# Recurrence steps on a common table of times, two clamps on GpSimd, and other first PSUM banks, in a one-core decoder layer

## The chip, the cores and the metric

The kernel runs on one core of a Trainium2 chip. A core has TensorE (PE, matmuls), VectorE (DVE), ScalarE (ACT), GpSimd (POOL) and SyncE (SP, which here starts transfers), each with its own queue of instructions that it works off in order; an instruction whose semaphore is not yet set holds up everything behind it in that queue. Matmul results land in PSUM banks of 128 x 512 float32, everything else lives in SBUF. The metric is the device time of one execution in microseconds (us). The kernel before takes 1142.49 us (median of 3 runs, 1142.37 to 1142.78).

## The reference

One layer of a hybrid decoder on a sequence of 1024 positions with 1024 channels, in float32: norm, one combined input projection, eight heads of dilated attention beside four heads of a gated linear recurrence (HGRN2), an output projection with a residual, and a gated MLP with a short convolution. The change is in the recurrence and in the projections that feed it:

```python
def hgrn2_mixer(q, f, i, lb):              # 4 heads, 128 wide, chunks of 64
    qf = silu(q)
    forget = lb + (1 - lb) * sigmoid(f)
    key, log_f = 1 - forget, log(forget)
    b = cumsum(log_f)                      # within a chunk
    q_dec, k_inv = qf * exp(b), key * exp(-b)
    A = tril(einsum(q_dec, k_inv))         # scores within a chunk
    o_intra = einsum(A, iv)
    k_end = key * exp(b_end - b)
    U = einsum(k_end, iv)                  # what a chunk adds to the state
    state = decay * state + U              # from chunk to chunk
    o_inter = einsum(q_dec, state)
    return o_intra + o_inter
```

The result is normalised per head, multiplied by a gate `silu(g)`, and goes with the attention's result into the output projection.

## The kernel before

**Products.** Each wide matrix product is made of three matmuls on a high and a low part of both operands (lines L514, L515, L516: high x high, low x high, high x low), with a 128 x 512 result. A pair of output tiles is made of seven such products (`pair_block`), by a scheme in the manner of Strassen's with sums of operands (names T1 to T4, B11, B21, B22). `product` yields a credit of 0.65 us for each three matmuls, and a filler (`fill.run(us)`) issues three at a time until the credit is used up. PE's program order is thus written by hand: what a step issues on PE stands where the filler had come to when the step was called. The order of the other engines' instructions is chosen by the framework's scheduler.

**First attention blocks.** The products for queries and keys (`qk_block`, evacuated by the copy L542 and the sums L544 to L556, then multiplied by a norm's row at L718 into `kp` and `qp`) are followed by scores `S` (L788), in groups of small matmuls between the wide ones; L797 applies the mask and takes the maximum of a score tile. `block_banks` names the PSUM bank that each product takes: `mm` in turn for the blocks from the second on. The banks have names by use (`mm`, `s`, `o`, `t`), each with its buffers.

**Recurrences.** Eight of them run: head h and half hf of the sequence, in the order (0,0), (0,1), (1,0), (1,1), (2,0), (3,0), (2,1), (3,1). While they run, the filler issues the wide products of the remaining projections and of the output projection. Each has five steps with wishes for time in a list `steps`, in units of 5.2 us of filler's credit:

1. start: `B`, the logarithm `A`, the running sum `C` (L1027), exponentials; `E` becomes q_dec and `B` k_inv. No matmul.
2. `psK` (L1044, four transposes of B into bank `t`, copied by ACT at L1052 into `kT`) and `psA` (L1049, L1050, eight narrow matmuls into bank `s`), masked by DVE at L1054 into `AT`.
3. `psU` (L1060, bank `s`), then the states: L1062, L1067, L1071 on DVE and L1068, L1072 on ACT; for hf 0 the last state is copied by POOL (`carry`, L1075).
4. `psO` (L1083, L1085, bank `o`), sums of squares (L1089, ACT), a reciprocal root (`rstd_part`: L369, L370, L371 on ACT, L372, L373 on DVE) and `on` (L1092, DVE).
5. `psT` (L1098, four transposes of `on` into bank `t`), then the gate's multiplication G (L1100, DVE).

I call what stands on PE between two wide matmuls a visit. Beside the recurrences a step `attn_stat` runs once for each half: four loads with squares (L968) and sums (L970), then, 4.0 units later, the sum `ass` over the partitions (L973, into a bank `t`) with `rstd_part` on it (so L369 and L372 there work on 128 x 512).

**Gates.** `q_out` and `g_last` evacuate q and the gate: a clamp at -40 into the tile `F` (L921, L928 on DVE), three ACT rows of a sigmoid on `F` (L859, L860, L861), and a multiplication on DVE (L923, L930). `F` has one buffer, so these chains follow each other one at a time.

Of the kernel before, what the change touches and what calls it, by code (L numbers as in the profile page):

```python
# [3 lines left out]

# [25 lines left out]
SHARED = 4  # L30
BIG = 1e30
PARTS = (13.2, 15.8)
STARTS = (1.7, 4.6, 7.6, 10.8, 14, 17, 19.4, 22.0)
SPLIT = 24.5
END = 27.8
STAT = (3.5, 6.8)
STAGES_AT = (1.8, 2.9, 4.1, 5.5)
PARKED = (5,)
PARK_I = (3, 4, 5, 5, 5, 6, 6, 6)

# [224 lines left out]
def hybrid_kernel(ctx: ExitStack, tc: tile.TileContext, xT, w_qk, w_tok, w_hg, w_out, w_up,  # L265
                  w_down, vecs, amask, hmask, out):
    nc = tc.nc
    PE, DVE, ACT, POOL = nc.tensor, nc.vector, nc.scalar, nc.gpsimd
# [132 lines left out]
    def bank(tag, name):  # L401
        return ps1.tile([P, H2], F32, tag=tag, name=name, bufs=2)
# [4 lines left out]
    at = at_cm.__enter__()  # L407
# [14 lines left out]
    def vtile(name):  # L422
        return at.tile([P, H2], F32, tag="vi", name=name, bufs=4)
# [135 lines left out]
    blocks, block_banks = [], [cycle(("mm",))]  # L559
# [136 lines left out]
    for t in TURN:  # L696
        x = vtile(f"it{t}")
        tok_out(ivd, t, x, V[t])

    def run(g):  # L700
        for _ in g:
            pass
# [18 lines left out]
    def qk_block(p):  # L721
        return pair_block(("qk", p), lambda m, hf: mtile(f"u{p}_{m}{hf}"), qk_evac(p))
# [7 lines left out]
    for hf in range(2):  # L730
        rms1_row(hf)
    run(first)
    block_banks[0] = cycle(("mm",))
    fill.add(*[qk_block(p) for p in range(1, 4)])
    fill.run(3.9)
    xp_cm.__exit__(None, None, None)
# [5 lines left out]
    if True:  # L742
# [29 lines left out]
        def scores(p, b):  # L772

            qp, kp = qk[p]
            far = 32 * max(b - 1, 0)
            near = P if b == 0 else 2 * P
            k0 = (b + 1) * P - near
            n = far + near
            S = [bank(("so" if b % 2 else "ss")[e], f"S{p}_{b}_{e}") for e in range(2)]
            rows = [slice(64 * e, 64 * e + 64) for e in range(2)]  # L780
            k4 = kp.rearrange("p (b r l) -> p r b l", r=4, l=32)
            for part in range(2 if far else 1):
                for r in range(4):
                    o = slice(32 * r, 32 * r + 32)
                    for e in range(2):
                        q = qp[rows[e], b * P + 32 * r : b * P + 32 * r + 32]
                        if part == 0:
                            PE.matmul(S[e][o, far:n], q, kp[rows[e], k0 : k0 + near], start=True, stop=True)  # L788
                        else:
                            PE.matmul(S[e][o, 0:far].rearrange("p (b l) -> p b l", l=32), q,  # L790
                                      k4[rows[e], r, 0 : b - 1], start=True, stop=True)
            m = mask[:, FAR - far :] if b else mask[:, FAR + P :]
            Ps = probs[p, b] = []
            for e in range(2):
                Pt = ab.tile([P, FAR + NEAR], F32, tag=f"P{e}", name=f"P{p}_{b}_{e}", bufs=3)
                st = at.tile([P, 16], F32, tag="st", name=f"st{p}_{b}_{e}", bufs=8)
                DVE.tensor_tensor_reduce(Pt[:, :n], S[e][:, :n], m, -(DH ** -0.5), BIG * 3,  # L797
                                         op0=ALU.add, op1=ALU.min, accum_out=st[:, 0:1])
                ACT.activation(Pt[:, :n], Pt[:, :n], AF.Exp, bias=st[:, 0:1], scale=-1.0, accum_out=st[:, 2:3])  # L799
                DVE.reciprocal(st[:, 3:4], st[:, 2:3])  # L800
                POOL.tensor_scalar(Pt[:, :n], Pt[:, :n], st[:, 3:4], 1.0, op0=ALU.mult, op1=ALU.mult)  # L801
                Ps.append(Pt)
# [55 lines left out]
        def sigmoid(dst, src):  # L858
            ACT.activation(dst, src, AF.Exp, scale=-1.0)  # L859
            ACT.activation(dst, dst, AF.Ln, bias=1.0)  # L860
            ACT.activation(dst, dst, AF.Exp, scale=-1.0)  # L861
# [17 lines left out]
        for x in slots[:LAG]:  # L879
            scores(*x)  # L880
            fill.run(1.5)
# [19 lines left out]
    with pool("hg", "right") as hg:  # L901
# [3 lines left out]
        def ht(tag, nm, bufs=1):  # L905
            return hg.tile([P, H2], F32, tag=tag, name=nm, bufs=bufs)
# [3 lines left out]
        def tile_of(kind, h, hf):  # L910
            tag, bufs = {"hf": ("A", 4), "hq": ("E", 5), "hg": ("GH"[h // 2], 4)}[kind]
            return ht(tag, f"{tag}{h}_{hf}", bufs)
# [5 lines left out]

        def q_out(h, hf, E):
            F = ht("F", f"F{h}_{hf}")  # L920
            DVE.tensor_scalar_max(F, E, -40.0)  # L921
            sigmoid(F, F)
            DVE.tensor_mul(E, E, F)  # L923
            gate.setdefault((h, hf), {}).update(E=E)

        def g_last(h, hf, g_):
            F = ht("F", f"Fg{h}_{hf}")
            DVE.tensor_scalar_max(F, g_, -40.0)  # L928
            sigmoid(F, F)
            DVE.tensor_mul(g_, g_, F)  # L930
            G[h, hf] = g_
# [31 lines left out]
        def attn_stat(hf):  # L963
            acc = ht("H", f"asq{hf}", 4)
            for c in range(4):
                x = ar[c % 2]
                nc.sync.dma_start(x, rawd[c, hf])
                ACT.activation(x if c else acc, x, AF.Square)  # L968
                if c:
                    DVE.tensor_add(acc, acc, x)  # L970
            yield
            ss = bank("t", f"ass{hf}")
            PE.matmul(ss, ones, acc, start=True, stop=True)  # L973
            R2.append(rstd_part(ht("R", f"R2_{hf}", 2), acc, ss, 1.0 / 512))
            yield

        def attn_parts(hf):
            hi, lo = spare(f"attn{hf}")
            for c in range(4):
                a = ring.raw(rawd[c, hf])  # L980
                DVE.scalar_tensor_tensor(a, a, col(V_AG + c), R2[hf], op0=ALU.mult, op1=ALU.mult)
                ACT.copy(hi[:, c], a)
                DVE.tensor_sub(lo[:, c], a, f32(hi[:, c]))
            return hi, lo
# [16 lines left out]
        for hf in range(2):  # L1001
            for kind, h in HG[0]:
                x = tile_of(kind, h, hf)
# [12 lines left out]
        def recur(h, hf):  # L1016
            A, E = (gate[h, hf].pop(x) for x in "AE")
            nm = f"{h}_{hf}"
# [18 lines left out]
            DVE.tensor_mul(E, E, C)  # L1037
            DVE.tensor_mul(B, B, A)
            yield
            psA = bank("s", f"psA{nm}")  # L1040
            psK = bank("t", f"psK{nm}")
            for c in range(4):
                s = slice(c * P, (c + 1) * P)
                PE.transpose(psK[:, s], B[:, s], ident)  # L1044


            for c in range(4):
                s, s1, s2 = slice(c * P, (c + 1) * P), slice(c * P, c * P + 64), slice(c * P + 64, (c + 1) * P)
                PE.matmul(psA[0:64, s], B[:, s1], E[:, s], start=True, stop=True)  # L1049
                PE.matmul(psA[64:128, s], B[:, s2], E[:, s2].unsqueeze(1).to_broadcast([P, 2, 64]), start=True, stop=True)  # L1050
            kT = ht("kT", f"kT{nm}")
            ACT.copy(kT, psK)  # L1052
            pA3 = psA.rearrange("p (c t) -> p c t", c=4)
            DVE.copy_predicated(AT, hm.unsqueeze(1).to_broadcast([P, 4, P]), pA3)  # L1054
            yield
# [2 lines left out]
            for c in range(n):  # L1058
                s = slice(c * P, (c + 1) * P)
# [4 lines left out]
            st = ht("rs_y", f"st{nm}").rearrange("p (c t) -> p c t", c=4)  # L1064
# [15 lines left out]
            for c in range(4):  # L1080
                s = slice(c * P, (c + 1) * P)
# [4 lines left out]
            sq, ss = ht("rs_m", f"hsq{nm}"), hg.tile([P, 12], F32, tag="sm", name=f"hss{nm}", bufs=2)  # L1086
            for c in range(4):
                s = slice(c * P, (c + 1) * P)
# [7 lines left out]
            for c in range(4):  # L1096
                s = slice(c * P, (c + 1) * P)
                PE.transpose(psT[:, s], on[:, s], ident)  # L1098
            g_ = G[h, hf]
# [6 lines left out]
        def split_rec(hf):  # L1106
            hi, lo = rec_parts[hf] = spare(f"rec{hf}")
            for h in range(NG):
                g_ = G.pop((h, hf))
                ACT.copy(hi[:, h], g_)  # L1110
                DVE.tensor_sub(lo[:, h], g_, f32(hi[:, h]))
# [13 lines left out]
        steps = []  # L1125
        attn_ops = {}

        def rec_steps(h, hf):
            chain = iter(())

            def first():
                nonlocal chain
                chain = recur(h, hf)
                next(chain)

            yield first
            while True:
                yield lambda: next(chain, None)

        for (h, hf), start in zip(((0, 0), (0, 1), (1, 0), (1, 1), (2, 0), (3, 0), (2, 1), (3, 1)),  # L1140
                                STARTS):
            steps += zip((start, *(start + x for x in STAGES_AT)), rec_steps(h, hf))
        for hf in range(2):
            stat = attn_stat(hf)
            steps += [(STAT[hf] + x, lambda stat=stat: next(stat, None)) for x in (0, 4.0)]
            steps.append((PARTS[hf], lambda hf=hf: attn_ops.update({hf: attn_parts(hf)})))
# [4 lines left out]
        def play(end):  # L1151

            nonlocal done
            while steps and steps[0][0] < end:
                at, f = steps.pop(0)
                fill.run(5.2 * (at - done))
                done = at
                f()
            fill.run(5.2 * (end - done))
            done = end  # L1160
# [55 lines left out]
        fill.add(*[out_block(*x) for x in OUT_BLOCKS[0]])  # L1216
        play(SPLIT)
        split_rec(0)
# [196 lines left out]
    with pool("ps2", "left", space=PSUM) as ps2:  # L1415
# [162 lines left out]
        for x, y in STAGES:  # L1578
# [11 lines left out]
            for k in range(NPAIR):  # L1590
                hi, lo = ring.get((("dn", x), k))
                ahi, alo = feed.get((y, k))
                for d in range(KS):
                    s = slice(d * P, (d + 1) * P)
# [102 lines left out]
```

## Time and profile before

| | |
|---|---|
| median of 3 runs | 1142.49 us |
| the profiled execution's own time | 1142.57 us |
| its span in the trace | 1140.6 us |
| PE, busy | 1127.5 us, 6404 matmuls |
| DVE, busy | 970.2 us |
| ACT, busy | 580.6 us |
| POOL, busy | 89.9 us |
| mean granted TensorE clock | 0.998 |

The span runs from the first to the last instruction that the profiler recorded; 1.97 us of the execution's own time lie around it. Busy time is the sum over an engine's instructions. Idle time of an engine that nothing waits for costs nothing. A line of a timeline gives start and length in us, the engine, the line of the kernel, the operation, out<-in, the tile's partitions x elements, how often, and in brackets how long the engine had been idle before it and what ended that.

### The profile page before, as it was taken

Reading aid. Unit: us, or ns where it says so; the run is one execution under the profiler, and the core shown is the slowest. Engines: PE = TensorE matmul, PEld = TensorE weight load, DVE = VectorE, ACT = ScalarE, POOL = GpSimd, SP = SyncE. Lnnn points to the kernel's source line nnn. Section 1 sums busy time; section 2 is a strip of 40 time slices with the busy share of each in tenths; the row PEclk is TensorE's granted clock in tenths of the full one; section 3 lists DMA queues with packets and bytes.
Section 4 is the critical chain, followed back from the end, with each engine's and each line's share of the span. In section 5 each row is a group of like instructions: output and inputs, shape, how many; then the busy total and the mean of one; then the engine's idle time right before and its main releaser. Section 6 shows DMA issues by size and latency. Waiting matters only on the chain.

```text
span 1140.6 us, 17940 instructions
## 1 busy us (share of the span) xinstructions
PE 1127.5 (99%) x6404; PEld 927.4 (81%) x6404; DVE 970.2 (85%) x1768; ACT 580.6 (51%) x1151; POOL 89.9 (8%) x107
## 2 busy tenths in 40 slices
PE   9999999999999999999999999999999999999996
PEld 8888677778878888888788888888888888888885
DVE  7687977778999985989999999888988789857987
ACT  7545545465788665564433434343434444444553
POOL 5200333330000002000000000000000000000000
PEclk9999999999999999999999999999999999999999
DMA  7147322224315542311233223322332376435532
GB/s 251 64 169 235 73 71 62 85 76 159 102 57 179 168 139 92 104 50 56 65 121 111 92 103 120 117 79 100 120 117 79 134 263 219 120 94 176 157 120 74
DMA packets 102088, 136.13 MB, mean 119 GB/s; under 512 B 25392, under 2 KB 44624, under 8 KB 102000
## 3 DMA queue, kind: packets, MB, share of 16 engines
q1 hardware_dynamic: 87712, 110.33, 31.6%
q10 hardware_dynamic: 14288, 24.67, 5.8%
q8 instruction: 50, 0.82, 0.3%
q14 instruction: 38, 0.31, 0.1%
HBM read 100.20 MB, written 34.76 MB: 118 GB/s over the span
## 4 chain that ended last, share of the span: by engine, by line
PE 93%; DVE 5%; DMA 1%; issue 1%; ACT 0%; DVEq 0%; ACTq 0%
PE p L1298 11%; PE p L1297 11%; PE p L1296 11%; PE w L514 5%; PE w L515 4%; PE w L516 4%; PE ds L1595 3%; PE ds L1597 3%; PE ds L1596 3%; PE po L514 3%; PE po L516 3%; PE po L515 3%; PE da L1597 2%; PE da L1595 2%; PE da L1596 2%; PE S L788 2%
## 5 line engine op out<-in xcount | busy, mean ns | idle before, releaser
L102 ACT CAST whi<-raww 128x512 fp32r<-128x512 f32 x253 | 154.5, 618 | 209.3 <-PE p L1297 75.4
L104 DVE TENSOR_TENSOR wlo<-raww,whi 128x512 fp32r<-128x512 f32 x254 | 176.9, 699 | 23.1 <-ACT whi L102 21.5
L102 ACT CAST whi<-r 128x512 fp32r<-128x512 f32 x70 | 43.6, 623 | 82.6 <-PE ds L1596 46.2
L104 DVE TENSOR_TENSOR wlo<-r,whi 128x512 fp32r<-128x512 f32 x70 | 48.0, 687 | 18.9 <-ACT whi L102 18.9
L1596 PE MATMUL ds<-flo,whi 128*128 128x512 f32 x160 | 62.3, 389 | 0.0
L1595 PE MATMUL ds<-fhi,whi 128*128 128x512 f32 x160 | 62.2, 389 | 0.0
L1296 PE MATMUL p<-b1h,whi 128*128 128x512 f32 x160 | 62.2, 389 | 0.0
L1297 PE MATMUL p<-b1l,whi 128*128 128x512 f32 x160 | 62.2, 389 | 0.0
L1298 PE MATMUL p<-b1h,wlo 128*128 128x512 f32 x160 | 62.2, 389 | 0.0
L1597 PE MATMUL ds<-fhi,wlo 128*128 128x512 f32 x160 | 62.2, 389 | 0.0
L801 POOL TENSOR_SCALAR P<-P,st 128x128 f32<-128x128 f32 (+7 forms) x64 | 47.1, 742 | 97.2 <-DVE st L800 77.1
L1569 POOL TENSOR_TENSOR facc<-facc,sqf 128x256 f32<-128x256 f32 x2 | 1.5, 735 | 670.9 <-ACT sqf L1568 670.9
L104 DVE TENSOR_TENSOR flo<-rawf,fhi 128x512 fp32r<-128x512 f32 x70 | 48.1, 687 | 4.0 <-ACT fhi L102 4.0
L102 ACT CAST fhi<-rawf 128x512 fp32r<-128x512 f32 x70 | 43.1, 616 | 13.2 <-PE p L1298 5.0
L1325 ACT ACTIVATE cv<-cv 128x512 f32<-128x512 f32 x44 | 27.8, 633 | 41.6 <-DVE cv L1318 41.6
L799 ACT ACTIVATE P<-P,st 128x128 f32<-128x128 f32 (+7 forms) x64 | 35.7, 559 | 25.6 <-DVE st L797 25.6
L1318 DVE SCALAR_TENSOR_TENSOR cv<-g,vec,cv 128x511 f32<-128x511 f32 (+2 forms) x92 | 44.8, 492 | 3.4 <-ACT cv L1315 3.1
L1595 PE MATMUL da<-fhi,whi 128*128 128x512 f32 x120 | 46.7, 389 | 0.0
L1596 PE MATMUL da<-flo,whi 128*128 128x512 f32 x120 | 46.7, 389 | 0.0
L1597 PE MATMUL da<-fhi,wlo 128*128 128x512 f32 x120 | 46.7, 389 | 0.0
L797 DVE CUSTOM_DVE_ANT_0 P<-S,mask 128x128 f32<-128x128 f32 (+7 forms) x64 | 28.8, 486 | 8.7 <-PE S L790 6.6
L1597 PEld LDWEIGHTS ds<-fhi,wlo 128*128 128x128 f32 x160 | 30.0, 188 | 6.3
(589 smaller groups left out, 3411.3 us busy)
## 6 DMA issues: line engine op xcount, KB each, us to landing
raww<-in_w_up_dram SPq DMA_DIRECT2D x88, 256.0 KB, 2.9
rawf<-spT SPq DMA_DIRECT2D x40, 256.0 KB, 2.8
r<-in_w_down_dram SPq DMA_DIRECT2D x40, 256.0 KB, 3.5
spB<-a ACTq DMA_DIRECT2D x30, 256.0 KB, 2.2
spT<-t ACTq DMA_DIRECT2D x30, 256.0 KB, 2.1
rawf<-spB SPq DMA_DIRECT2D x30, 256.0 KB, 2.8
raww<-in_w_out_dram SPq DMA_DIRECT2D x28, 256.0 KB, 2.8
raww<-in_w_hg_dram SPq DMA_DIRECT2D x24, 256.0 KB, 2.8
```

Of the source, the lines that this page charges most:

```text
L102: self.pin(self.high(hi[:, :w], raw))
L104: self.pin(low.tensor_sub(lo[:, :w], raw, f32(hi[:, :w])))
L514: PE.matmul(ps, a[0], b[0], start=start, stop=False)
L515: PE.matmul(ps, a[0], b[1], start=False, stop=False)
L516: PE.matmul(ps, a[1], b[0], start=False, stop=stop)
L801: POOL.tensor_scalar(Pt[:, :n], Pt[:, :n], st[:, 3:4], 1.0, op0=ALU.mult, op1=ALU.mult)
L1296: PE.matmul(ps, hi[:, s], bhi, start=(start and n == 0), stop=False)
L1297: PE.matmul(ps, hi[:, s], blo, start=False, stop=False)
L1298: PE.matmul(ps, lo[:, s], bhi, start=False, stop=(stop and n == len(rhs) - 1))
L1595: PE.matmul(ps[d], hi[:, s], ahi, start=(k == 0), stop=False)
L1596: PE.matmul(ps[d], hi[:, s], alo, start=False, stop=False)
L1597: PE.matmul(ps[d], lo[:, s], ahi, start=False, stop=(k == NPAIR - 1))
```

## The change

Three things change at once.

- **Times of the recurrence's steps.** `STARTS` and `STAGES_AT` (the same offsets from each start) become `LEAD` (the starts) and `BEATS` (one table of 18 times that all recurrences share). Recurrence j has psK just ahead of beat 2j, psA just behind it, psU just ahead of beat 2j+1, psO at beat 2j+2 and psT at beat 2j+3. As beat 2j+2 is that of psK and psA of the next recurrence and beat 2j+3 that of its psU, one visit now holds psK of j, psO of j-1 and psA of j, and the next one psU of j and psT of j-1. `play` rounds a time to a tenth, so that nothing is filled in between. `recur` yields once more, between psK and psA. `STAT[0]` goes from 3.5 to 2.7, so that the two steps of `attn_stat(0)` come earlier among the others, and `SPLIT` from 24.5 to 24.0.
- **Clamps.** The 14 clamps of `q_out` (six) and `g_last` (eight) go from DVE to POOL.
- **Banks.** The first two products after the first block go to banks `t` instead of `mm`, and of the first two score tiles S the second goes to `t` instead of `s`.

```diff
+LEAD = (1.7, 4.6, 7.5, 10.4, 13.3, 16.2, 19.1, 22.0)
+BEATS = (3.2, 4.6, 6.2, 7.5, 9.1, 10.4, 12.0, 13.3, 14.9, 16.2, 17.8, 19.1, 20.7, 22.0, 23.6, 24.9, 26.5, 27.8)
-STARTS = (1.7, 4.6, 7.6, 10.8, 14, 17, 19.4, 22.0)
-SPLIT = 24.5
+SPLIT = 24.0
-STAT = (3.5, 6.8)
-STAGES_AT = (1.8, 2.9, 4.1, 5.5)
+STAT = (2.7, 6.8)
...
-    block_banks[0] = cycle(("mm",))
+    block_banks[0] = chain(('t', 't'), cycle(("mm",)))
...
-            S = [bank(("so" if b % 2 else "ss")[e], f"S{p}_{b}_{e}") for e in range(2)]
+            S = [bank(("so" if b % 2 else "ss" if (p, b) != (0, 0) else 'st')[e], f"S{p}_{b}_{e}") for e in range(2)]
...
-            DVE.tensor_scalar_max(F, E, -40.0)
+            POOL.tensor_scalar_max(F, E, -40.0)
...
-            DVE.tensor_scalar_max(F, g_, -40.0)
+            POOL.tensor_scalar_max(F, g_, -40.0)
...
-            psA = bank("s", f"psA{nm}")
             psK = bank("t", f"psK{nm}")
             for c in range(4):
                 s = slice(c * P, (c + 1) * P)
                 PE.transpose(psK[:, s], B[:, s], ident)
-
+            kT = ht("kT", f"kT{nm}")
+            ACT.copy(kT, psK)
+            yield
+            psA = bank("s", f"psA{nm}")
...
-        for (h, hf), start in zip(((0, 0), (0, 1), (1, 0), (1, 1), (2, 0), (3, 0), (2, 1), (3, 1)),
-                                STARTS):
-            steps += zip((start, *(start + x for x in STAGES_AT)), rec_steps(h, hf))
+        ats = [[(LEAD[j], 0.0), (BEATS[2 * j], -0.02), (BEATS[2 * j], 0.02), (BEATS[2 * j + 1], -0.02), (BEATS[2 * j + 2], 0.0),
+                (BEATS[2 * j + 3], 0.0)] for j in range(8)]
+        for (h, hf), at in zip(((0, 0), (0, 1), (1, 0), (1, 1), (2, 0), (3, 0), (2, 1), (3, 1)), ats):
+            steps += zip((x + y for x, y in at), rec_steps(h, hf))
...
+                at = round(at, 1)
                 fill.run(5.2 * (at - done))
```

What this moves in the engines' queues is shown where psU of the second recurrence stands on PE, with what belongs to that on the other engines. A row gives the line, the operation, out<-in (a number behind a name tells instances apart) and the shape. PE before, from the wide matmul ahead of the first recurrence's psT (`psT_0`) to psU of the second recurrence:

```order
L516 MATMUL w_3837<-B11h,wlo_3671 128x512
L1098 MATMUL psT_0_3844<-ident,on_0_3739 128x128 x4
L514 MATMUL w_3837<-B11h,whi_3670 128x512
L515 MATMUL w_3837<-B11l,whi_3670 128x512
L516 MATMUL w_3837<-B11h,wlo_3671 128x512
L514 MATMUL w_3837<-B11h,whi_3670 128x512
L515 MATMUL w_3837<-B11l,whi_3670 128x512
L516 MATMUL w_3837<-B11h,wlo_3671 128x512
L514 MATMUL w_3862<-T2h,whi_3698 128x512
L515 MATMUL w_3862<-T2l,whi_3698 128x512
L516 MATMUL w_3862<-T2h,wlo_3699 128x512
L1060 MATMUL psU_1_3866<-iv_1_3642,kT_1_3790 128x128 x3
```

Behind these three psU rows stands `ass`. PE of the changed kernel at the same place of the program, around `ass`, which now comes first:

```order
L514 MATMUL w_3801<-B22h,whi_3614 128x512
L515 MATMUL w_3801<-B22l,whi_3614 128x512
L516 MATMUL w_3801<-B22h,wlo_3615 128x512
L973 MATMUL ass_3808<-asq_3520,ones 128x512
L514 MATMUL w_3801<-B22h,whi_3614 128x512
```

and, with 21 wide matmuls between `ass` and it, the visit of psU of the second recurrence and psT of the first:

```order
L514 MATMUL w_3864<-T2h,whi_3698 128x512
L515 MATMUL w_3864<-T2l,whi_3698 128x512
L516 MATMUL w_3864<-T2h,wlo_3699 128x512
L1060 MATMUL psU_1_3868<-iv_1_3642,kT_1_3744 128x128 x3
L1098 MATMUL psT_0_3882<-ident,on_0_3771 128x128 x4
```

Before, psT_0 took a bank `t` ahead of `ass`, and `ass` took the one that psT_0 had filled; now `ass` takes the one that psK of the second recurrence had filled, and psT_0 the one that `ass` had filled, whose last reader is L372 on 128 x 512 (`asq`).

ACT of the changed kernel, from the last row of the q gate's sigmoid (`F_1`) to the last of the three rows of `rstd_part` on `ass`; `Fg_0` is the first recurrence's gate:

```order
L861 ACTIVATE F_1_3726<-F_1_3726 128x512
L371 ACTIVATE hss_0_3761<-hss_0_3761 128x4
L1020 ACTIVATE B_0_3888<-A_0_3580,lb 128x512
L1021 ACTIVATE A_0_3580<-A_0_3580,lb 128x512
L859 ACTIVATE Fg_0_3746<-Fg_0_3746 128x512
L369 ACTIVATE asq_3520<-ass_3808,eps 128x512
L860 ACTIVATE Fg_0_3746<-Fg_0_3746 128x512
L370 ACTIVATE R_0_3810<-asq_3520 128x512
L861 ACTIVATE Fg_0_3746<-Fg_0_3746 128x512
L371 ACTIVATE asq_3520<-R_0_3810 128x512
```

Before, the gate `Fg_0` was through ahead of all these rows, and L369 on `ass` stood among the sigmoid rows of a forget gate; now it stands behind L859 on `Fg_0`.

DVE of the changed kernel, from the multiplication by `F_1` (L923) to the last reader of `ass` (L372 on asq):

```order
L923 TENSOR_TENSOR E_1_3703<-E_1_3703,F_1_3726 128x512
L372 SCALAR_TENSOR_TENSOR hss_0_3761<-hss_0_3761 128x4
L951 TENSOR_TENSOR E_0_3680<-E_0_3680,R_90 128x512
L373 SCALAR_TENSOR_TENSOR hss_0_3761<-hss_0_3761 128x4
L1092 TENSOR_TENSOR on_0_3771<-psO_0_3752,hss_0_3761 128x512
L1027 SCALAR_TENSOR_TENSOR C_0_3893<-chunks,A_0_3580 128x512
L556 TENSOR_TENSOR A_1_3599<-w_3801,A_1_3599 128x512
L1031 TENSOR_TENSOR A_0_3580<-C_0_3893 128x512
L951 TENSOR_TENSOR A_1_3599<-A_1_3599,R_90 128x512
L930 TENSOR_TENSOR G_0_3387<-G_0_3387,Fg_0_3746 128x512
L372 SCALAR_TENSOR_TENSOR asq_3520<-ass_3808,asq_3520 128x512
```

The clamps that stood in this queue before are gone; L930 by `Fg_0` stands directly ahead of L372 on asq. On POOL they stand, in this order, behind the first `carry` copy:

```order
L1075 COPY carry_3637<-U_0_3628 128x128
L921 TENSOR_SCALAR F_1_3726<-E_1_3703 128x512
L928 TENSOR_SCALAR Fg_0_3746<-G_0_3387 128x512
L921 TENSOR_SCALAR F_0_3795<-E_0_3680 128x512
L928 TENSOR_SCALAR Fg_1_3983<-G_1_3406 128x512
```

Before, POOL had nothing between one `carry` copy and the next.

More of the change, by code (lines that the diff above doesn't have):

```diff
@@ L2 @@
 from contextlib import ExitStack
-from itertools import cycle
+from itertools import chain, cycle
 import concourse.bass as bass
@@ L1050, in recur @@
                 PE.matmul(psA[64:128, s], B[:, s2], E[:, s2].unsqueeze(1).to_broadcast([P, 2, 64]), start=True, stop=True)
-            kT = ht("kT", f"kT{nm}")
-            ACT.copy(kT, psK)
             pA3 = psA.rearrange("p (c t) -> p c t", c=4)
```

## The prediction

> **What bounds the kernel now.** I read the busy times first, then the chain of work that ended last, then what PE waits for in the whole span.
>
> ```profile
> PE 1127.5 (99%) x6404; PEld 927.4 (81%) x6404; DVE 970.2 (85%) x1768; ACT 580.6 (51%) x1151; POOL 89.9 (8%) x107
> PE 93%; DVE 5%; DMA 1%; issue 1%; ACT 0%; DVEq 0%; ACTq 0%
> ```
>
> ```profile
> PE warm L433 <- DVE eps L295: 1.1, 1, 1.1
> PE w L514 <- ACT u L542: 1.0, 1, 1.0
> PE ass L973 <- DVE G L1100: 0.9, 1, 0.9
> PE S L788 <- DVE st L797: 0.5, 1, 0.5
> ```
>
> PE is busy 1127.5 of 1140.6 us, so a change that neither adds nor removes a matmul, as this one, can gain only what PE loses to waits and to the beginnings and ends of visits. The list of PE's waits is the whole of the first: four waits, of which the one at the start of the kernel (warm) is not touched. The other three, 2.4 us together, all lie at places that the change reaches. On the other side stands DVE. In the 30 us around the first recurrences (columns: PE, PEld, DVE, ACT, POOL busy with counts, clock, DMA share, GB/s) it is as full as PE:
>
> ```profile
> 294.00:304.00 10.00, 10.00 (x53) 8.53 (x53) 9.96 (x20) 8.21 (x22) 2.76 (x1) 1.00 0.22 58
> 304.00:314.00 10.00, 10.00 (x60) 8.14 (x59) 10.00 (x18) 7.14 (x20) 0.00 (x0) 1.00 0.24 74
> 314.00:324.00 10.00, 9.09 (x47) 7.31 (x45) 9.86 (x21) 9.44 (x21) 0.00 (x0) 1.00 0.16 54
> ```
>
> PE keeps busy there only as long as it does not need a DVE result sooner than today. That is where a price can arise.
>
> **First banks: -1.6 us.** Rows of PE, ACT and DVE around the first two scores:
>
> ```profile
> 117.53 0.39 PE L516 MATMUL w<-B11h,wlo 128*128 128x512 f32 x1
> 118.93 0.50 PE L514 MATMUL w<-T2h,whi 128*128 128x512 f32 x1 [1.01 <-ACT u L542]
> 119.26 0.40 PE L515 MATMUL w<-T2l,whi 128*128 128x512 f32 x1
> 118.30 0.58 ACT L542 COPY u<-w 128x512 f32<-128x512 f32 x1
> 115.36 1.89 DVE L104 TENSOR_TENSOR wlo<-raww,whi 128x512 fp32r<-128x512 f32 x3
> 118.36 1.07 DVE L718 TENSOR_TENSOR kp<-u,R 128x512 f32<-128x512 f32 x1
> 122.83 0.40 PE L516 MATMUL w<-B21h,wlo 128*128 128x512 f32 x1
> 123.68 0.67 PE L788 MATMUL S<-kp,qp 64*32 64x256 f32 x16 [0.46 <-DVE st L797]
> 123.24 0.28 DVE L797 CUSTOM_DVE_ANT_0 P<-S,mask 128x128 f32<-128x128 f32 x1
> ```
>
> Wide matmuls follow each other at 0.23 us, so the T2 product could begin at 117.76. It begins at 118.93, when the copy L542 at 118.30 has emptied the bank of the product before, which it is to take. In a bank `t` it needs its weights alone, and three of these were split by 117.25 (the x3 row). That is 118.93 - 117.76 = 1.17 us. Next the scores need kp, done at 119.43; with nine wide matmuls ahead of them they come at 117.76 + 9 x 0.23 = 119.8, so kp does not replace the wait, and L542 has long freed what it held. Then S at 123.68, which waited 0.46 for L797 to clear the bank of the first scores, has a bank more. All that is 1.63; I take 1.6. L797 itself waits for its mask rather than for PE, so scores that come sooner may queue on it a little: bounds -1.1 (the second wait stays, 0.46 less) and -1.7.
>
> **`ass` of the first half: -0.9 us.**
>
> ```profile
> 314.01 0.83 PE L1060 MATMUL psU<-iv,kT 128*128 128x128 f32 x6
> 315.75 1.13 PE L973 MATMUL ass<-asq,ones 128*128 128x512 f32 x2 [0.91 <-DVE G L1100]
> 314.95 0.74 DVE L1100 SCALAR_TENSOR_TENSOR G<-psT,vec,G 128x512 f32<-128x512 f32 x1
> ```
>
> `ass` takes the bank that psT filled, and G reads psT until 315.69. In the changed order `ass` stands ahead of that psT and takes psK's bank, emptied by an ACT copy; the wait of 0.91 goes. Bounds 0 (its sums are late instead) and -0.9.
>
> **Visits: -0.4 us.** Two pairs of rows each with its own visit, and one visit that the kernel of before already shares:
>
> ```profile
> 420.28 0.83 PE L1060 MATMUL psU<-iv,kT 128*128 128x128 f32 x6
> 420.86 0.48 PE L514 MATMUL po<-attn0h,whi 128*128 128x512 f32 x1
> 422.34 0.60 PE L1098 MATMUL psT<-ident,on 128*128 128x128 f32 x4
> 422.70 0.48 PE L514 MATMUL po<-attn0h,whi 128*128 128x512 f32 x1
> 439.24 0.60 PE L1098 MATMUL psT<-ident,on 128*128 128x128 f32 x4
> 440.26 0.48 PE L514 MATMUL po<-rec0h,whi 128*128 128x512 f32 x1
> ```
>
> Apart they cost 0.58 + 0.36 = 0.94 us, plus twice the slower first wide matmul behind a visit (a gap of 0.33 in place of 0.23, as at 118.93 and 119.26), so 1.14. Together they cost 1.02 + 0.10 = 1.12. A visit saved is worth 0.02 to 0.1 us, its restart; I take 0.04. PE's order has 31 visits by the recurrences before and 20 after, so eleven times 0.04 is 0.44, bounds 0.2 and 1.1. No matmul goes.
>
> **psT_0 now waits for `ass`: +1.2 us.** This is the new wait. In the order, psU of the second recurrence has as many rows ahead of it as before, with `ass` in place of psT_0, so it comes at about 314.1 on the clock of before, and psT_0 is wanted at 314.1 + 0.58 = 314.7. Its bank is free when DVE's L372 has read `ass`. `ass` itself is early (21 wide matmuls, 4.8 us, ahead of psU), but ACT's L369 on it is queued behind L859 on Fg_0, and that waits for POOL's clamp, which waits for the one buffer F, which L923 on F_1 releases. The rows of that chain today:
>
> ```profile
> 306.39 0.69 DVE L951 TENSOR_TENSOR E<-E,R 128x512 f32<-128x512 f32 x1
> 308.27 0.42 DVE L921 TENSOR_SCALAR F<-E 128x512 f32<-128x512 f32 x1
> 309.73 0.62 ACT L859 ACTIVATE F<-F 128x512 f32<-128x512 f32 x1
> 311.99 0.63 ACT L861 ACTIVATE F<-F 128x512 f32<-128x512 f32 x1
> 312.81 0.69 DVE L923 TENSOR_TENSOR E<-E,F 128x512 f32<-128x512 f32 x1
> 317.62 0.67 ACT L369 ACTIVATE asq<-ass,eps 128x512 f32<-128x512 f32 x1
> 321.37 0.68 DVE L372 SCALAR_TENSOR_TENSOR asq<-ass,asq 128x512 f32<-128x512 f32 x1
> ```
>
> And the prices for a clamp of 128x512 on POOL, which no row shows:
>
> ```profile
> L459 POOL TENSOR_TENSOR sums<-sums,sq 128x512 f32<-128x512 f32 x14 | 22.6, 1642 | 23.4 <-ACT sq L457 23.4
> L801 POOL TENSOR_SCALAR P<-P,st 128x448 f32<-128x448 f32 x8 | 6.4, 801 | 9.3 <-DVE st L800 9.3
> 298.86 2.76 POOL L1075 COPY carry<-U 128x128 f32<-128x128 f32 x1 [42.68 <-PE w L516]
> 408.08 0.29 POOL L1075 COPY carry<-U 128x128 f32<-128x128 f32 x1 [18.79 <-DVE U L1071]
> ```
>
> The nearest is L801, the same operation on 448 columns at 0.80; I take 0.8, from DVE's 0.42 below to the carry copy's 2.76 above. L951 ends about 306.6 (a few short rows fewer ahead of it than at 306.39). Clamp to 307.4; three sigmoid rows and a cast at a pitch of 0.53, with two short ones, to 310.0; L923 to 310.7; clamp to 311.5; six ACT rows (L859, L369, L860, L370, L861, L371) at 0.53 to 314.7; L372 behind L930 to 315.5. Six hand-overs at some 0.07 each make it 315.9, so PE waits 315.9 - 314.7 = 1.2. With clamps of 0.42 it waits 0.4; with 1.64, 2.9; with 2.76, 5.1. Behind the waiting psT on PE stand the wide products, and everything is late by as much.
>
> On DVE the 14 clamps leave some 0.4 each, 5.6 us in all; in the stretch above DVE has no idle time, so this helps the rows behind, but L923 now stands at the queue's head until POOL and ACT have come round (five rows, 3.0 us, between L951 and L923, against 3.4 of chain). I cost it at nothing: PE has no other wait on DVE there, and an early DVE is not waited for.
>
> **`ass` of the second half: +0.3 us.** It still takes psT's bank and now stands nine wide matmuls, 2.1 us, behind it; G has to come within that, on a DVE whose next rows are due about when PE arrives. I count 0 to 1.0, and take 0.3.
>
> **Sum.** -1.6 - 0.9 - 0.4 + 1.2 + 0.3 = -1.4. The profiled execution took 1142.57 (span 1140.6 and 1.97 around it), 0.08 over the median of the three runs; so 1142.57 - 1.4 - 0.08 = 1141.1.
>
> **A rule of the skill against this change.** The carry copy of 128x128 took 0.29 at 408.08 but 2.76 at 298.86, in the full stretch of DVE. The Trainium skill, page "SBUF — State Buffer", section "Who interferes with whom", says that a DVE instruction with two SBUF inputs contends with a GpSimd instruction that reads SBUF, and that the one that started first keeps the shared ports for the whole of it. The direction agrees with 0.29 and 2.76; the size does not, since by that rule a copy waits for one DVE instruction (0.69, so about 1.0), not for several. By it each clamp would take 0.8 + 0.7, the wait of psT_0 would be 2.6, and the sum 0.0.
>
> **The rivals.**
> - *No new wait (0.27).* The chain runs ahead of psT_0: DVE, relieved of its clamps, reaches L951 1 us sooner, or a clamp takes 0.42. Then -1.6 - 0.9 - 0.5 = -3.0: 1139.5. For it: only 1.2 us decide. Against it: ten links in a row.
> - *One wait for another (0.17).* Clamps of some 1.5 us, blocked by DVE's rows or blocking them: 2.6 at psT_0, 1.0 at the second `ass`: -2.9 + 3.6 = +0.7, so 1143.2. For it: 298.86. Against it: L801 at 0.80, taken while DVE worked too. This is what the skill's rule comes to.
> - *Slower (0.11).* Both clamps of the chain are held off as the carry copy was, 2.76 each, by DVE's unbroken rows from 294 to 324: 5.1 at psT_0, 1.0 at the second `ass`: -2.9 + 6.1 = +3.2, so 1145.7. It decides from clamps of 2.3 on, where the sum passes +2.3.
> - *The first banks do nothing (0.05).* T2's weights or S's mask come last at the same time anyway: +1.2 + 0.3 - 0.9 - 0.4 = +0.2, 1142.7.
>
> **How the numbers follow.** The forecast (0.40) is 1140.2 to 1142.5 by the bounds of its terms. A difference under 0.2%, 2.3 us, is about what a measurement of this kernel can't tell from no change, so the border of faster is 1140.2 and of slower 1144.8. Faster is the first rival, 0.27; slower the third, 0.11; the rest, 0.62, is the same. The range leaves out the slower rival and what lies below the sum of all gains: 1139.2 to 1144.0.
>
> **What would show it.** The list of PE's waits: `w <- u L542` and `S <- st L797` gone (first banks); `ass <- G L1100` gone or now at the second half; a new `psT <- asq L372` of about 1.2 at 313 (the chain). The POOL groups L921 and L928 with a mean of 0.8 (price), above 1.5 for the rivals. PE's busy time down by some 0.4 (visits). I am wrong if PE waits at a place not named here, for instance at psK or at a wide product whose weights DVE splits too late.

## The result and the profile after

The changed kernel takes 1150.87 us (median of 5 runs, 1150.51 to 1152.73) against 1142.67 (five runs of the kernel before): a ratio of 1.0074, with a 95% interval of 1.0063 to 1.0085. The forecast was 1141.1 with 1139.2 to 1144.0 as the range; the kernel is 8.2 us slower, where 1.4 us faster was the likeliest. The profiled execution took 1150.51, with a span of 1148.6.

I start again with the engines' busy times and the list of PE's waits (engine, line and tile, what it waited for: us in total, times, longest), now of the changed kernel:

```profile
PE 1129.3 (98%) x6404; PEld 928.8 (81%) x6404; DVE 968.8 (84%) x1754; ACT 580.7 (51%) x1151; POOL 110.8 (10%) x121
PE psT L1098 <- DVE on L1092: 2.9, 1, 2.9
PE psT L1098 <- DVE asq L372: 2.6, 1, 2.6
PE ass L973 <- DVE G L1100: 1.6, 1, 1.6
PE warm L433 <- DVE eps L295: 1.0, 1, 1.0
PE w L514 <- DVE A L556: 0.7, 1, 0.7
PE po L514 <- DVE h L1193: 0.6, 1, 0.6
PE p L1300 <- DVE wlo L104: 0.2, 1, 0.2
```

The waits of `w` on u and of S on L797 are gone, and `ass` of the first half no longer waits: what was to go, went. In its place stand the two new waits that the prediction named (psT on asq, the second `ass` on G), both longer than it said, and four that it did not name. The waits sum to 9.6 us against 3.5 before. PE's busy time has grown by 1.8 although no matmul was added. 6.1 and 1.8 make the 8.0 us by which the span grew, to the rounding of the rows.

Nearly all of the 1.8 belongs to the clock. The windows of the changed kernel around the wait of psT on asq (columns: PE's busy time with its count, granted clock, DMA share, GB/s):

```profile
313.00:316.00 3.00, 0.45 (x5) 1.00 0.00 0
316.00:319.00 3.00, 3.00 (x10) 0.50 0.28 92
319.00:322.00 3.00, 3.00 (x14) 0.93 0.00 1
```

Behind the wait PE ran at half its clock to 319.3. About 3.3 us at half the clock cost some 1.6 us.

Next, the chain of work in that stretch (start, length of its part of the chain, engine, tile, line), from the q of the second recurrence (E, L951) to the psT that waited:

```profile
303.18 0.61 DVE E L951
...
304.03 2.33 POOL F L921
306.37 0.63 ACT F L859
...
308.32 0.53 ACT F L861
...
308.96 0.69 DVE E L923
...
309.74 1.94 POOL Fg L928
311.70 0.63 ACT Fg L859
312.33 0.58 ACT asq L369
...
313.94 0.53 ACT Fg L861
...
314.56 0.69 DVE G L930
315.26 0.61 DVE asq L372
...
315.91 1.07 PE psT L1098 x4
```

This is link for link the chain that the prediction wrote down. Its rows on ACT and DVE have the lengths that the rows of before gave. Two do not: the clamps, 2.33 and 1.94 us where the sum has 0.8 each. All 14 clamps of the changed kernel, grouped (count, busy us, mean ns, idle before):

```profile
L921 POOL TENSOR_SCALAR F<-E 128x512 f32<-128x512 f32 x6 | 11.2, 1866 | 47.8 <-DVE E L951 30.9 <-DVE hss L373 13.2 <-DVE G L930 3.7
L928 POOL TENSOR_SCALAR Fg<-H 128x512 f32<-128x512 f32 x4 | 6.7, 1681 | 20.9 <-DVE H L930 13.3 <-DVE H L951 7.6
L928 POOL TENSOR_SCALAR Fg<-G 128x512 f32<-128x512 f32 x4 | 6.5, 1617 | 14.5 <-DVE E L923 11.1 <-DVE hss L372 3.4
```

24.4 us for 14, a mean of 1.74 against 0.42 on DVE (5.9 us for the 14 before). What waits for them first is ACT, all 20 us of it (in the list of waits of the same kernel):

```profile
ACT F L859 <- POOL F L921: 10.9, 6, 3.1
ACT Fg L859 <- POOL Fg L928: 9.2, 5, 3.5
```

and behind L859 on ACT's queue stand rows of other work. In the same stretch DVE, which had hardly any idle time before, stood still for 1.97 us for a cast of weights (L102) that stood behind L859 on ACT's queue:

```profile
308.35 0.69 DVE L104 TENSOR_TENSOR wlo<-raww,whi 128x512 fp32r<-128x512 f32 x1 [1.97 <-ACT whi L102]
```

So an engine that was full lost time to the engine that was meant to relieve it. Two theories remained: the clamps on POOL (A), or the common times themselves, which put psT behind `ass` and closer behind psO (B).

### The profile page after: what moved, and what is told of

Its sections match the earlier page's. It is cut to its first block, busy times and chain, and to the rows that moved or that the text cites. A ratio compares the mean times of both kernels' runs of the same rounds, so it can differ in the third digit from the quotient of the medians.

```text
span 1148.6 us, 17951 instructions
## 1 busy us (share of the span) xinstructions
PE 1129.3 (98%) x6404; PEld 928.8 (81%) x6404; DVE 968.8 (84%) x1754; ACT 580.7 (51%) x1151; POOL 110.8 (10%) x121
## 4 chain that ended last, share of the span: by engine, by line
PE 88%; DVE 8%; ACT 1%; DMA 1%; issue 1%; POOL 1%; DVEq 0%; SPq 0%; POOLq 0%; ACTq 0%
PE p L1300 11%; PE p L1299 11%; PE p L1298 11%; PE w L514 5%; PE w L516 4%; PE w L515 4%; PE ds L1597 3%; PE ds L1598 3%; PE ds L1599 3%; PE da L1597 2%; PE da L1598 2%; PE da L1599 2%; PE po L514 2%; PE po L516 2%; PE po L515 2%; PE S L788 2%
## 5 line engine op out<-in xcount | busy, mean ns | idle before, releaser
L102 ACT CAST whi<-raww 128x512 fp32r<-128x512 f32 x253 | 154.6, 617 | 210.4 <-PE p L1299 72.9
L102 ACT CAST whi<-r 128x512 fp32r<-128x512 f32 x70 | 43.6, 623 | 84.4 <-PE ds L1598 46.7
L801 POOL TENSOR_SCALAR P<-P,st 128x128 f32<-128x128 f32 (+7 forms) x64 | 46.4, 730 | 96.0 <-DVE st L800 90.7
L102 ACT CAST fhi<-rawf 128x512 fp32r<-128x512 f32 x70 | 43.2, 617 | 13.5 <-PE p L1300 5.0
L1298 PEld LDWEIGHTS p<-b1h,whi 128*128 128x128 f32 x160 | 30.0, 188 | 6.3
```

The source lines that it names most:

```text
L102: self.pin(self.high(hi[:, :w], raw))
L1298: PE.matmul(ps, hi[:, s], bhi, start=(start and n == 0), stop=False)
```

## The experiments

**The parts one by one.** Four kernels beside runs of the kernel before. First the changed kernel without the move of the clamps:

```diff
-            POOL.tensor_scalar_max(F, E, -40.0)
+            DVE.tensor_scalar_max(F, E, -40.0)
...
-            POOL.tensor_scalar_max(F, g_, -40.0)
+            DVE.tensor_scalar_max(F, g_, -40.0)
```

> The changed kernel with all 14 clamps back on DVE; the common times and the first banks stay. Theory A (the clamp on POOL, 1.5 to 2.3 us apiece at the head of chains, makes the new waits): the waits of psT on asq and on `on`, of the second ass on G and of the wide products go or fall under 0.5 each, and the gains stay: 1139.5 to 1141.0 us. Theory B (the common times themselves make them, because psT stands behind ass in its bank and closer behind psO): the waits of psT and of ass stay above 1.5 each, 1147 us or more. A mixture would lie between, and the list of PE's waits tells which wait belongs to which.

1140.27 us against 1142.52, a ratio of 0.998 (0.9971 to 0.999): theory A. The same kernel once more:

> The kernel with the common times and the first banks, clamps on DVE, once more and in five rounds, as the version that was ahead of both kernels: 1140.3 us, 0.998 of the time before, with the interval below 1. If its first figure was luck: 0.9987 or more, no better than the banks alone.

1140.26 against 1142.71, 0.9978 (0.9969 to 0.9987), in 11 runs. PE's waits in that second profile are two, and one of them is the start of the kernel:

```profile
PE warm L433 <- DVE eps L295: 1.1, 1, 1.1
PE ass L973 <- DVE G L1100: 0.5, 1, 0.5
```

psT, in the same order on PE and behind the same `ass`, does not wait at all. This version is ahead of both kernels, by 2.4 us of the one before.

PE's order is the same in both versions, but that of DVE and ACT, which the scheduler chooses, is not. With the clamps on DVE, L372 on asq begins at 311.54, ahead of the gate's multiplication L930 at 313.35; in the changed kernel it stands behind it (314.56 and 315.26 in the chain above). So this difference of 10.6 us is that of the clamps' place with all that the scheduler makes of it.

The reverse, the kernel before with nothing but the clamps on POOL:

```diff
-            DVE.tensor_scalar_max(F, E, -40.0)
+            POOL.tensor_scalar_max(F, E, -40.0)
...
-            DVE.tensor_scalar_max(F, g_, -40.0)
+            POOL.tensor_scalar_max(F, g_, -40.0)
```

> The kernel before with the 14 clamps on POOL and nothing else. Theory A: the clamps take 1.5 us or more here too, DVE's rows run into them, and PE gets new waits without the common times: 1145 to 1150 us. Theory B: psT and ass have 2 to 6 us of room in the old order, so the longer chains are hidden: within 1 us of 1142.7.

1152.80 against 1142.52, 1.0091 (1.0076 to 1.0106), 10.3 us more and beyond what theory A expected. In the old order the waits fall elsewhere; the longest three of PE there:

```profile
PE po L514 <- DVE h L1191: 3.2, 1, 3.2
PE w L514 <- DVE A L544: 1.5, 1, 1.5
PE psO L1085 <- ACT st L1072: 1.3, 2, 1.2
```

The two kernels together rule B out for the loss. With the common times and the clamps on DVE there is no loss, and with the old times and the clamps on POOL there is the whole of it. The common times decide where PE waits for a late chain, and not that it is late. The cost of the clamps is about the same in both orders, 10.3 here and 1150.87 - 1140.27 = 10.6 there.

The other first banks alone, on the kernel before:

```diff
-    block_banks[0] = cycle(("mm",))
+    block_banks[0] = chain(("t", "t"), cycle(("mm",)))
...
-            S = [bank(("so" if b % 2 else "ss")[e], f"S{p}_{b}_{e}") for e in range(2)]
+            S = [bank(("so" if b % 2 else "ss" if (p, b) != (0, 0) else "st")[e], f"S{p}_{b}_{e}") for e in range(2)]
```

> The kernel before with the other first banks alone. Both theories: the waits w<-u (1.0) and S<-st (0.5) are gone and nothing else moves, 1.6 us less: 1141.1 us. If the gain is lost behind (a DVE-bound stretch that takes it back): 1142.7 us.

1140.87 against 1142.52, 0.9988 (0.9978 to 0.9997): 1.65 us, as forecast (the interval allows 0.3 to 2.5), and the waits of `w` and S are gone from the list. The common times are then worth 0.6 us beyond the banks (1140.87 - 1140.27, measured together), which the overlapping intervals do not tell from nothing.

Last, the changed kernel with `ass` of the first half behind psT again:

```diff
-STAT = (2.7, 6.8)
+STAT = (3.5, 6.8)
```

> The changed kernel with STAT[0] back at 3.5, so that ass of the first half stands behind psT of the first recurrence and does not hand it its bank. Theory A and B differ little: psT's wait of 2.6 on asq goes, and with it the 3.3 us at half the TensorE clock behind it if that stretch belongs to the wait (1.7 us): 1146.6 us. If the clock fell for another reason, 1148.3 us. The waits of the third psT on `on` (2.9) and of the second ass (1.6) stay.

1153.26, 1.0094 (1.0079 to 1.0109): 6.7 us over the 1146.6 that I expected, and slower than the changed kernel. The same psT now waits for something else, and longer:

```profile
317.11 1.08 PE L1098 MATMUL psT<-ident,on 128*128 128x128 f32 x4 [4.58 <-DVE on L1092]
```

`on` comes out of the same two engines' queues, behind L923. With the bank out of the way, the late chain holds up PE at its next link. The wait on asq was the place, not the cause.

**Which clamps.** The changed kernel with only one of the two lines back on DVE: g clamps back (q on POOL), and q clamps back (g on POOL).

> The changed kernel with the eight clamps of g_last back on DVE, so that only the six of q_out are on POOL. If each clamp costs by itself, the q clamps carry 6/14 of the 10.6 us between both clamps' places: 1144.8 us. If it is the two in a row through the one buffer F that make the waits (theory of the chain), breaking it takes most of the loss away: under 1142.5 us, with psT's wait on asq under 1.0.

> The changed kernel with the six clamps of q_out back on DVE, so that only the eight of g_last are on POOL. By the share of 8/14: 1146.3 us. By the theory of the chain: under 1142.5 us, with the third psT's wait on `on` left at most, since the clamp of a gate stood on ACT's queue ahead of the rows that `on` needs.

1148.96 against 1142.75 (1.0061, 1.0046 to 1.0076) with the six q clamps; 1145.35 (1.0022, 1.0013 to 1.0032) with the eight g clamps. Over 1140.27 that is 8.7 and 5.1, more together than the 10.6 of both. Neither expectation holds: the six cost more than the eight, and neither alone is cheap, so two of POOL's clamps in a row through the one buffer are not needed for the loss. (The eight come near their share, 1145.35 against 1146.3, with runs from 1143.56 to 1146.75.) With q alone the longest wait of PE is one that the changed kernel does not have, psK on B (2.2 us; it is 0.7 with g alone): its row,

```profile
325.18 0.96 PE L1043 MATMUL psK<-ident,B 128*128 128x128 f32 x4 [2.18 <-DVE B L1038]
```

is a start of the next recurrence that is late behind the q gate. Ahead of it one of the six clamps, at 314.80, took 4.00 us, longer than any of the changed kernel (1.48 to 2.33); L859 on ACT waited 3.77 for it, and L923 on DVE 3.18 behind that.

**The price of a clamp by itself.** A small kernel with none of the layer's work: 13 rows on POOL four times over, with DVE idle (but for the first clamp, beside which the last rows of its preparation ran), then beside DVE rows with two SBUF inputs, beside DVE clamps with one SBUF input, and beside DVE rows that read one input from PSUM.

> A kernel that computes nothing of the layer: on GpSimd, for 128x512, three clamps (max with a constant), three multiplications by a column (the operation of L801), three by a constant, two copies, and two copies of 128x128, four times over: with DVE idle, then beside DVE rows with two SBUF inputs, beside DVE clamps with one SBUF input, and beside DVE rows with one PSUM input. Price theory (the clamp itself is dear on GpSimd): 1.5 us with DVE idle already, the multiplication by a column 0.8. Contention theory (GpSimd is held off by DVE's rows): 0.7 to 0.8 with DVE idle, and 1.5 to 2.3 only beside DVE rows with two SBUF inputs, where DVE's rows grow too.

Its rows on POOL, for the clamps (L80, max), the multiplications by a column (L82) and the small copies (L88); start and length of the whole group of three or two. First with DVE idle, then beside two SBUF inputs, then beside PSUM:

```profile
4.92 5.00 POOL L80 TENSOR_SCALAR F<-A 128x512 f32<-128x512 f32 x3 [4.49 <-DVE A L74]
9.99 2.27 POOL L82 TENSOR_SCALAR M<-A,sc 128x512 f32<-128x512 f32 x3
15.43 0.65 POOL L88 COPY D<-A 128x128 f32<-128x128 f32 x2
16.42 5.09 POOL L80 TENSOR_SCALAR F<-A 128x512 f32<-128x512 f32 x3 [0.35 <-DVE A L101]
21.59 4.50 POOL L82 TENSOR_SCALAR M<-A,sc 128x512 f32<-128x512 f32 x3
31.11 1.44 POOL L88 COPY D<-A 128x128 f32<-128x128 f32 x2
78.33 4.62 POOL L80 TENSOR_SCALAR F<-A 128x512 f32<-128x512 f32 x3 [16.78 <-DVE A L101]
83.04 2.27 POOL L82 TENSOR_SCALAR M<-A,sc 128x512 f32<-128x512 f32 x3
```

Undisturbed, the maximum takes 4.62 / 3 = 1.54 us (the second and third one with DVE idle took 3.05 together), and the multiplication 2.27 / 3 = 0.76: the same name of operation, shape and engine, half the time. 0.76 is about what the row L801 had promised, but for another arithmetic. Contention is real beside it: next to two-input rows the multiplication doubles (4.50 / 3 = 1.50) and the small copy goes from 0.33 to 0.72, while the long maximum gains little (1.70). DVE's clamps, with their one SBUF input, disturb too: beside them the maximum took 1.81 and the multiplication 1.06. DVE's side of it, its rows with two SBUF inputs (L91) and with one from PSUM (L97):

```profile
L91 DVE TENSOR_TENSOR W<-B,Y 128x512 f32<-128x512 f32 x44 | 31.3, 786 | 0.0
...
L97 DVE TENSOR_TENSOR W<-ps,Y 128x512 f32<-128x512 f32 x44 | 26.4, 675 | 0.0
```

The 44 rows with PSUM took 26.4 us, the 44 with two SBUF inputs 31.3, 4.9 more over the 16 us in which POOL worked beside them. It is POOL and not the second input that lengthens them: 19 rows took 15.8 us while POOL worked, 0.83 each, and 25 took 14.7 once it had stopped, 0.59 each.

**Price or trip.** The changed kernel with a cheaper operation in the same place; the clamp is left out:

```diff
-            POOL.tensor_scalar_max(F, E, -40.0)
+            POOL.tensor_scalar(F, E, 1.0, 0.0, op0=ALU.mult, op1=ALU.add)
...
-            POOL.tensor_scalar_max(F, g_, -40.0)
+            POOL.tensor_scalar(F, g_, 1.0, 0.0, op0=ALU.mult, op1=ALU.add)
```

> The changed kernel with GpSimd's maximum with -40 replaced by a multiplication by 1.0, an operation that took 0.67 us with DVE idle and 1.02 beside its two-input rows, where the maximum took 1.5 and 1.7; the clamp is left out, everything else stays. If the price of the maximum is the step that failed (0.8 in the prediction's sum): the rows L921 and L928 average 0.7 to 1.1, psT's wait on asq falls from 2.6 to about 1, the others in proportion, and the time is 1141 to 1143.5 us. If it is the trip through POOL itself (two hand-overs, DVE's queue stopped at L923) rather than the length of the row: over 1147 us.

1144.29 against 1142.71, 1.0013 (1.0004 to 1.0022): 0.8 above what the price theory expected and far below the other. The rows of POOL now average 1.00 (q) and 0.75 to 0.82 (g), and psT's wait on asq is 1.67. Every row of DVE and ACT stands in the same order as in the changed kernel, so the two programs differ in POOL's operation alone. So of the 10.6 us the price of the maximum is 1150.87 - 1144.29 = 6.6, and 4.0 remain with a row whose mean is near the 0.8 that I had assumed. (PE's busy time is 1127.4 here and 1129.3 there, so 1.9 of the 6.6 are time at a lower clock.) In the chain of psT_0 even the multiplication took 1.46 and 1.07, where three of its kind took 2.02 undisturbed in the small kernel (L84, 0.67 each) and 3.07 beside DVE's two-input rows (1.02 each): in the full stretch of DVE the cheap row grew as well. Two more kernels took that rest apart: only four columns on POOL, in place, with the sigmoid reading the source itself, and nothing on POOL.

```diff
-            POOL.tensor_scalar_max(F, E, -40.0)
-            sigmoid(F, F)
+            POOL.tensor_scalar(E[:, 0:4], E[:, 0:4], 1.0, 0.0, op0=ALU.mult, op1=ALU.add)
+            sigmoid(F, E)
...
-            POOL.tensor_scalar_max(F, g_, -40.0)
-            sigmoid(F, F)
+            POOL.tensor_scalar(g_[:, 0:4], g_[:, 0:4], 1.0, 0.0, op0=ALU.mult, op1=ALU.add)
+            sigmoid(F, g_)
```

> The changed kernel with GpSimd's row reduced to a multiplication by 1.0 of four columns, in place, ahead of the sigmoid, which then reads the source itself; the clamp is left out. The trip through GpSimd stays, its length goes. Length theory (what is lost grows with the time that the row takes: 1140.3 at 0.42 on DVE, 1144.3 at 0.85, 1150.9 at 1.73): at most 1140.5 us. Hand-over theory (the 4 us that were left with a cheap row belong to the two extra hand-overs and the stopped queues): 1143 to 1144.3 us.

> The same without GpSimd's row: the sigmoid reads the source, no clamp anywhere (it is left out). The floor for any place of the clamp: the gains of the banks and the common times, and DVE's 5.9 us of clamps gone. If DVE's share decides nothing any more, as without waits on PE: 1139.8 to 1140.3 us, the same as with the clamps on DVE; if DVE's full stretch still costs PE something: 1139.3 us or less.

1142.22 with four columns (0.9995, 0.9985 to 1.0004) and 1139.79 without (0.9974, 0.9965 to 0.9984), both against 1142.64. The trip with so small a row costs 2.4 us, between the two expectations; the order of some rows on DVE and ACT differs between these two, and that is in it. Even rows of four columns are not always short (the groups of that kernel, on q, on the gates of the first two heads, and on those of the last two):

```profile
L921 POOL TENSOR_SCALAR E<-E 128x4 f32<-128x4 f32 x6 | 3.6, 594 | 55.3 <-DVE hss L372 21.9 <-DVE E L951 17.4 <-PE psT L1098 16.0
L928 POOL TENSOR_SCALAR G<-G 128x4 f32<-128x4 f32 x4 | 2.8, 712 | 32.6 <-DVE G L951 32.6
L928 POOL TENSOR_SCALAR H<-H 128x4 f32<-128x4 f32 x4 | 1.2, 288 | 20.0 <-DVE H L951 20.0
```

Means of 0.59 and 0.71 us against 0.29 for the last heads, and single rows from 0.19 to 1.17, for the same four columns. The ladder of all versions with banks and common times (from several sets of runs, whose kernels of before differ by 0.2): nothing 1139.79, clamp on DVE 1140.27, four columns on POOL 1142.22, multiplication 1144.29, maximum 1150.87. And the 14 x 0.42 = 5.9 us of DVE that the move takes off it are worth about 0.5 us when they go for nothing, with intervals that overlap.

**A last touch.** The wait of the second `ass` in the fast version:

```diff
-STAT = (2.7, 6.8)
+STAT = (2.7, 7.2)
```

The clamps are on DVE here.

> The changed kernel with all clamps on DVE and STAT[1] at 7.2 in place of 6.8, which puts the second ass 18 wide matmuls behind the psT whose bank it takes, in place of nine: its wait of 0.5 on G goes. 1139.8 us against 1140.3 without. If the wait only moves to the next reader of the bank, no difference.

1141.10 against 1142.75, 0.9987 (0.9977 to 0.9996): no gain. The wait of `ass` is gone; two others take its place, 0.52 and 1.00:

```profile
376.06 0.66 PE L1098 MATMUL psT<-ident,on 128*128 128x128 f32 x4 [0.52 <-DVE on L1092]
395.99 0.50 PE L514 MATMUL po<-attn1h,whi 128*128 128x512 f32 x1 [1.00 <-DVE h L1193]
```

## Why the prediction was wrong, by its own steps

- **First banks, -1.6:** right. 1.65 us alone, with both waits gone, though the interval (0.3 to 2.5) is wider than the term's bounds.
- **`ass` of the first half, -0.9:** right; it has no wait in the changed kernel.
- **Visits, -0.4:** not shown. PE's busy time is 1127.5 in the kernel with the banks alone, and 1126.3 and 1127.3 in the two profiles with the common times too; these two are of one kernel and differ by more than the term. PE's waits on `ass` go from 1.1 to 0.5 with the common times, and that is already all of the 0.6 us that these are worth.
- **psT_0 waits for `ass`, +1.2:** the mechanism was right to the link, and the term was mis-sized. The failed step is the price of the clamp: "The nearest is L801, the same operation on 448 columns at 0.80; I take 0.8". It is the same operation by name, and another arithmetic: a maximum takes 1.54 undisturbed and 2.33 and 1.94 in this chain. With these the prediction's own sum gives 1.2 + 1.53 + 1.14 = 3.9; measured were 2.55, since L951 ended at 303.79, some 1.5 earlier than I had it (306.6, less the 1.3 by which psT is wanted sooner). From the end of L951 to psT the chain took 12.1 us where the sum has 9.3; 2.7 of these 2.8 are the two clamps. The end of the range there (2.76) covered the price; the choice within it was wrong.
- **DVE's queue, "I cost it at nothing":** failed. That "an early DVE is not waited for" holds for an early one; DVE became late. L859 on ACT stands in wait of POOL for 20 us, ACT's casts stand behind it, and DVE behind these. The waits that the prediction did not name (psT on `on` 2.9, `w` on A 0.7, po on h 0.6, p on wlo 0.2) come to 4.4. Two of them remain with the multiplication in the clamp's place, 1.4 for the first and 0.7 for the third. With the two waits that were named, 1.67 and 0.72 there, PE waits 3.0 us more than the prediction's 1.2 and 0.3, which is about the 3.2 by which that kernel lies over the forecast of 1141.1. So a price of 0.8 alone would not have saved the forecast. Not every one of these waits is due to POOL: p on wlo is 0.2 with the clamps on DVE too (in the first of the two runs), and po on h was 1.0 with the clamps on DVE and the second `ass` moved.
- **The second `ass`, +0.3 (0 to 1.0):** 1.6 here, over its bound; 0.5 with the clamps on DVE, within it.
- **Left out altogether:** the clock. A wait of 2.55 us was followed by 3.3 us at half the clock, some 1.6 us more.
- **The account.** The profiled execution lies 9.4 us over the forecast. The two named waits are 2.6 longer than in the sum, the four others make 4.4, and PE's busy time is 2.2 over the 1127.1 that the visits were to leave: 9.2 together.
- **The rivals.** The time is that of the slower rival, and beyond its +3.2, but not by its mechanism alone. It decides from clamps of 2.3 on, and the two in the chain had a mean of 2.14. By its prices the nearest is "one wait for another": clamps of some 1.5 and a wait of 2.6 at psT_0 were just what was measured (1.74 as the mean of all, 2.55). It put the whole at only 1143.2, because it too left out the waits that were not named and the clock. That the slower rival had the right side is therefore in part luck. Of their reasons, "blocked by DVE's rows" was half right, as the clamps are slow by themselves (1.54) before DVE's rows hold them off (to 2.33). The rule of the Trainium skill that I weighed ("SBUF — State Buffer", "Who interferes with whom") is borne out in its direction by the small kernel, for rows with two SBUF inputs (31.3 against 26.4). That the port is held for a whole row is not what the changed kernel shows: a two-input row of DVE began and ended at its usual length inside a clamp of 1.49 us that started at 369.20:

```profile
369.20 1.49 POOL L921 TENSOR_SCALAR F<-E 128x512 f32<-128x512 f32 x1 [4.82 <-DVE E L951]
369.68 0.69 DVE L951 TENSOR_TENSOR A<-A,R 128x512 f32<-128x512 f32 x1
```

What stays open: why the maximum takes twice the multiplication (it is also the one row of the small kernel's arithmetic with a single operation, where the others have two, and no run tells the two apart); how the 4.0 us that remain with the multiplication divide between the hand-overs, the rows that grow beside DVE's and the other order of rows on DVE and ACT; and why the two halves of the clamps cost more apart (8.7 and 5.1) than both together (10.6), where the order of the rows differs again.

## What to carry to other kernels

A price for an operation on another engine must come from a row with the same arithmetic in the same form, and not merely the same instruction name; where no such row is there, a kernel of a few rows gives it before the change is made. Taking work off a full engine is worth only what that engine's lateness costs today (here about 0.5 us for all of it), while the hand-over stands at the head of two queues, and everything behind it in them pays. Waits for a chain that is late move from link to link when one of them is removed (from asq to `on`, from `ass` to psT): shorten the chain, or leave it.

## What the runs showed of the hardware that I had not expected

Besides the maximum on GpSimd: PE's granted clock fell to half at some waits of 2 to 5 us, and not in order of their length. Waits of 2.18 (q clamps on POOL, psK), 2.55 (changed kernel, psT), 3.19 (clamps alone, po) and 4.58 (`ass` at 3.5, psT) were followed by 3.3 to 7 us at a granted clock of 0.50, or fell into it while they lasted; waits of 2.48 (g clamps on POOL, `ass`), 2.89 (changed kernel, the fourth psT, which my expectations call the third) and 3.08 (`ass` at 3.5, the same psT) were not. The windows of the 2.89 one in the changed kernel:

```profile
383.00:386.00 3.00, 0.60 (x5) 1.00 0.78 231
386.00:389.00 3.00, 3.00 (x15) 1.00 0.50 166
```

The same kernel seems to go either way: of the four executions with the clamps alone on POOL, one had a mean clock of 0.998 and took 1150.99 us, and two had 0.994 and took 1152.79 and 1152.81 (the fourth took 1154.37 at 0.944). So such a wait cost some 1.6 us beyond itself in the changed kernel, or nothing. No run varied the length of a wait alone, so what decides between the two stays open.
